# Turning half of the residual by transposing transfers at four stage entries of a fused decoder trunk

## The chip, the core and the metric

The kernel runs on one core of a Trainium2 chip. The core has TensorE (PE in the profile, with its weight loads as PEld), VectorE (DVE), ScalarE (ACT), GpSimd (POOL), and SyncE (SP), which here only issues transfers. All engines run side by side, each through its own list of instructions in order, and wait for one another by semaphores. Transfers that SP issues go through one hardware queue (q1 in the profile), those of POOL through a software queue (q0), and both are served by the same 16 DMA engines. The metric is the device time of one execution in microseconds (us).

## What is computed

A residual stream of 256 tokens and 1024 channels passes two layers; each is a half-step FFN, a mixer, and a half-step FFN, and every one of these six sub-layers reads a normed copy of the stream and adds its normed output to it. The mixer of the first layer is a recurrent block, that of the second is attention whose keys, values and forget gates come from the stream between the layers.

```python
def rms_norm(x, g):
    xf = x.astype(jnp.float32)
    y = xf * lax.rsqrt(jnp.mean(xf * xf, axis=-1, keepdims=True) + EPS)
    return (y * g.astype(jnp.float32)).astype(x.dtype)

def swiglu(x, w_gate, w_up, w_down):
    return (jax.nn.silu(x @ w_gate) * (x @ w_up)) @ w_down

    for layer in range(DEPTH):
        if layer == N_A_LAYERS:
            k, v, c = shared_kv(h, kv_norm_g, w_kv, w_fgate, b_fgate)
        f = swiglu(rms_norm(h, ffn1_pre_g[layer]), ffn1_w_gate[layer], ffn1_w_up[layer], ffn1_w_down[layer])
        h = h + 0.5 * rms_norm(f, ffn1_post_g[layer])
        hn = rms_norm(h, mix_pre_g[layer])
        ...
        h = h + rms_norm(m, mix_post_g[layer])
        f = swiglu(rms_norm(h, ffn2_pre_g[layer]), ffn2_w_gate[layer], ffn2_w_up[layer], ffn2_w_down[layer])
        h = h + 0.5 * rms_norm(f, ffn2_post_g[layer])
    return h
```

All of it is float32. The attention of 16 heads adds to each logit a bias from the running sum of the forget gates, and masks keys later than the query.

## The kernel before

**Tiles.** The 256 tokens are two token tiles, t = 0 and t = 1, of 128. The residual lies in SBUF as `h[0]` and `h[1]`, 128 tokens on the partitions by 1024 channels. A product needs its input the other way round, channels on the partitions: eight k tiles of 128 channels each, numbered 0 to 7. `xhi` and `xlo` hold them, an upper part in a rounded 32-bit format that TensorE takes at full rate and the remainder. Each weight is split in the same way into `whi` (ScalarE, L173) and `wlo` (VectorE, L177), and each product is three matmuls: upper by upper, upper by lower, lower by upper.

**Units.** The weights come in units of 512 KB or so: `load_raw` issues the transfer on SP, `split` makes the two parts. Five raw tiles and nine pairs of parts stand in rotation. The list `items` holds all units in order, and `run` walks it with token tile 0 about seven units ahead of token tile 1. A unit of a projection holds two k tiles and is six matmuls for one token tile. After each unit `tick` is called; `defer(n, f)` has `f` written out n ticks later. TensorE keeps the written order; the other engines' lists are ordered by a scheduler, except where `keep_in_program_order` pins an instruction and `high_priority` pulls a group forward.

**Stage inputs.** When the last product of a sub-layer is done for a token tile, `enter` takes the sum of squares (ScalarE, L205), multiplies by the gain (VectorE, L284), and adds to the residual (L297, one instruction for each half of 512 channels). Three or four ticks later `inputs` turns the new residual: `to_tp` writes four TensorE transposes for each half (L226) into a PSUM bank of the group `gt`; `to_x` then multiplies by the gain of the next norm (VectorE, L234), copies the upper part (ScalarE, L235), and subtracts for the lower part (VectorE, L240). The root of the mean square is left out there and applied to the products' results. There are four such entries:

- entry A: recurrent block to the second FFN of layer 0
- entry B: that FFN to layer 1, where the residual is turned for two inputs, `xhi`/`xlo` and, with another gain, `zhi`/`zlo` for keys, values and gates
- entry C: the first FFN of layer 1 to attention, whose query projection comes first
- entry D: attention to the last FFN

(The entry into the recurrent block goes another way, by `normed_x`.) After entry C the units of the query projection alternate with attention's first steps in an order written by hand (`ATT_ORDER`): logits of token tile 0 (TensorE L1165, then VectorE L1174 with L1178 and L1179 for the row maxima, then ScalarE L1181 for the exponentials, then VectorE L1187 and L1188 for the norm), transposes of the probabilities (L1194), products with the values (L1208). POOL loads 2 MB of bias for token tile 1 at that point (L1009).

**Planes.** The FFN's hidden tiles are already turned by transfer, 48 times: POOL splits the 32-bit words into two planes of 16 bits (L527), SP issues one transposing transfer (`DMA_TRANSPOSE`, L535), and POOL joins the planes again (L540). `planes` (L212), `swap` (L216) and `join` (L220) are the same three steps as functions, used for keys and queries.

Of the kernel before, what the change touches and what calls it, by code (L numbers as in the profile page):

```python
# [17 lines left out]
P = 128  # L18
# [25 lines left out]
def trunk_kernel(ctx: ExitStack, tc: tile.TileContext, A: dict, out: bass.AP):  # L44
# [184 lines left out]
    def x_upper(tp, dest, n):  # L229

        gi, xh, xl = dest
        xg = hpool.tile([P, 4, P], F32, tag="t1", name=nm("xg"), bufs=2)
        g = gT[:, gi + 4 * n:gi + 4 * n + 4].unsqueeze(2).to_broadcast([P, 4, P])
        nc.vector.tensor_tensor(xg, tp.rearrange("p (a b) -> p a b", a=4), g, ALU.mult)  # L234
        nc.scalar.activation(xh[:, 4 * n:4 * n + 4, :], xg, AF.Copy)  # L235
        return xg

    def x_lower(xg, dest, n):
        gi, xh, xl = dest
        nc.vector.tensor_tensor(xl[:, 4 * n:4 * n + 4, :], xg, xh[:, 4 * n:4 * n + 4, :].bitcast(F32), ALU.subtract)  # L240

    def to_x(tps, dest):

        with tc.high_priority():
            xg = [x_upper(tps[n], dest, n) for n in range(2)]
            for n in range(2):
                x_lower(xg[n], dest, n)

    def to_x_tiles(tps, dest):

# [15 lines left out]
    def stat(t):  # L266
        ss = new_ss()
        square_sum(h[t], ss[:, 0:1])
        rs[t] = rstd_of(ss, 1)

    def enter(t, dests, pf, gb, half, last=False, normed=False, wait=3):

        f = 1.0 / 16 if half else 1.0 / 32
        ss = new_ss()
# [27 lines left out]
        if last:  # L302
            return

        def inputs():
            tps = [to_tp(h[t], n) for n in range(2)]
            for dest in dests:
                to_x(tps, dest)
            stat(t)

        def norm():
            with tc.high_priority():
# [179 lines left out]
    def ahead(i, fn):  # L492
# [5 lines left out]
            return prep()  # L498
        items[i] = (both, work)

    def ffn_items(pool_of, wg, wu, wd, post_g, next_dests, last=False, normed=False):
        hid = {}
        sil = {}
# [63 lines left out]
        ahead(i0 + 24, load_gb)  # L567

        def post_down(t, accs):
            enter(t, next_dests(t), accs, box["gb"], True, last, normed)  # L570

        row_items(wd, [P] * 22, lambda t, k: (hid[t][0][:, k, :], hid[t][1][:, k, :]), post_down, 4 if last else 2)
        return i0
# [645 lines left out]
    def post_q(n):  # L1219
        return lambda t, ps: heads_T(ps, t, n, HD ** -0.5, att["q"][t])  # L1220

    for n in range(2):
        proj_items(A["attn_w_q"][0], n * 512, 512, main_x, post_q(n))
    n_q[0] = len(items)
    row_items(A["attn_w_o"][0], [P] * 8, lambda t, k: (att["oh"][t][:, k, :], att["ol"][t][:, k, :]),
              lambda t, accs: enter(t, [main_dest(GI[("ffn2", 1)], t)], accs, gbox["mix1"], False, wait=4),
              rows0=1, late=True)
    ahead(n_q[0] + 2, load_gb("mix1", A["mix_post_g"][1]))
    n_att = len(items)
# [240 lines left out]
```

## Time and profile before

| | us |
|---|---|
| median of 3 runs | 966.03 (965.65 to 968.62) |
| profiled execution, its own time | 965.92 |
| span of that execution in the trace | 964.2 |
| VectorE busy in the span | 640.7 |
| ScalarE busy | 527.6 |
| POOL busy | 218.2 |

The time around the span (1.7 us) is the start and end of the program. Times of day in the rows below are us from the span's start. A row of the timeline gives start, length, engine, line, operation, what is written and read, the shape, how many, and in brackets how long the engine had been idle and what ended the idle time. A matmul's end is modelled: the next one starts before it, so the pace of TensorE is read from start to start.

### The profile page before, as it was taken

How to read it: one execution, taken by the hardware profiler on the slowest of the kernel's cores; microseconds unless marked ns; L12 is line 12 of the kernel's file. 1: busy time of each engine (PE TensorE's matmuls, PEld its weight loads, DVE VectorE, ACT ScalarE, POOL GpSimd, SP SyncE). 2: the span in 40 equal slices, each digit the busy share in tenths (PEclk: the TensorE clock that was granted, in tenths of full speed). 3: DMA queues.
4: the chain of work that ended last, by engine and by line, in shares of the span. 5: the costliest groups of instructions: out<-in, count | busy, mean ns of one | idle time of the engine just before them, and what ended most of it. 6: DMA issues, size and time to landing. Idle time of an engine off the chain costs nothing.

```text
span 964.2 us, 12866 instructions
## 1 busy us (share of the span) xinstructions
PE 955.9 (99%) x4575; PEld 791.3 (82%) x4575; DVE 640.7 (66%) x845; ACT 527.6 (55%) x750; POOL 218.2 (23%) x221
## 2 busy tenths in 40 slices
PE   9999999999999999999999999999999999999997
PEld 6888888898878888888898888888887788888886
DVE  6658674678997666664686566665488876666642
ACT  7546453568886555443565455444366855444431
POOL 2712330130001323230003522234022012232200
PEclk9999999999999999999999999999999999999999
DMA  8787995475346787775558979878773468777731
GB/s 286 226 258 225 256 284 197 142 228 163 119 123 219 209 236 211 205 242 196 135 182 278 253 219 258 230 216 265 226 256 97 133 199 236 207 222 233 223 109 44
DMA packets 148934, 198.79 MB, mean 206 GB/s; under 512 B 67166, under 2 KB 85958, under 8 KB 148742
## 3 DMA queue, kind: packets, MB, share of 16 engines
q1 hardware_dynamic: 146182, 191.06, 65.6%
q0 software_dynamic: 2080, 6.38, 2.1%
q8 instruction: 36, 0.59, 0.2%
q10 hardware_dynamic: 608, 0.53, 0.2%
q14 instruction: 28, 0.23, 0.1%
HBM read 182.19 MB, written 3.16 MB: 192 GB/s over the span
## 4 chain that ended last, share of the span: by engine, by line
PE 95%; DVE 2%; ACT 1%; issue 1%; POOL 0%; DMA 0%; POOLq 0%; DVEq 0%; ACTq 0%
PE mm L428 16%; PE mm L429 16%; PE mm L432 16%; PE mm L183 13%; PE mm L185 13%; PE mm L184 13%; PE gt L795 2%; PE mm L1305 1%; PE mm L190 1%; PE mm L191 1%; PE mm L192 1%; PE gt L226 1%; ACT pe L1181 1%; DVE wlo L177 0%; PE tr L127 0%
## 5 line engine op out<-in xcount | busy, mean ns | idle before, releaser
L177 DVE TENSOR_TENSOR wlo<-raw,whi 128x1024 fp32r<-128x1024 f32 (+5 forms) x329 | 418.0, 1276 | 230.7 <-ACT whi L173 228.3
L173 ACT ACTIVATE whi<-raw 128x1024 fp32r<-128x1024 f32 (+5 forms) x329 | 341.9, 1045 | 308.6 <-PE mm L432 119.2
L428 PE MATMUL mm<-whi,xhi 128*128 128x512 f32 x656 | 256.6, 391 | 0.0
L429 PE MATMUL mm<-wlo,xhi 128*128 128x512 f32 x656 | 255.5, 389 | 0.0
L432 PE MATMUL mm<-whi,xlo 128*128 128x512 f32 x656 | 202.1, 389 | 0.0
L428 PEld LDWEIGHTS mm<-whi,xhi 128*128 128x128 f32 x656 | 123.2, 188 | 25.9 <-issue 0.7
L432 PEld LDWEIGHTS mm<-whi,xlo 128*128 128x128 f32 x656 | 123.1, 188 | 25.8 <-DVE xlo L240 0.2
L429 PEld LDWEIGHTS mm<-wlo,xhi 128*128 128x128 f32 x656 | 123.2, 188 | 25.4 <-DVE wlo L177 0.3
L183 PE MATMUL mm<-whi,hhi 128*128 128x512 f32 x352 | 137.2, 390 | 0.0
L185 PE MATMUL mm<-whi,hlo 128*128 128x512 f32 x352 | 137.0, 389 | 0.0
L184 PE MATMUL mm<-wlo,hhi 128*128 128x512 f32 x352 | 136.9, 389 | 0.0
L540 POOL COPY pl<-prod 128x1024 uint16<-128x1024 uint16 (+1 forms) x48 | 69.9, 1456 | 174.4 <-DMA prod<-pl 174.4
L527 POOL COPY pl<-prod 128x1024 uint16<-128x1024 uint16 (+1 forms) x48 | 66.3, 1382 | 151.9 <-DVE prod L524 86.8
L183 PEld LDWEIGHTS mm<-whi,hhi 128*128 128x128 f32 x352 | 66.1, 188 | 13.7
L185 PEld LDWEIGHTS mm<-whi,hlo 128*128 128x128 f32 x352 | 66.1, 188 | 13.7
L184 PEld LDWEIGHTS mm<-wlo,hhi 128*128 128x128 f32 x352 | 66.1, 188 | 13.6
L198 POOL TENSOR_SCALAR nv<-ss 128x1 f32<-128x1 f32 x22 | 9.6, 437 | 268.7 <-ACT junk L205 268.7
L524 DVE SCALAR_TENSOR_TENSOR prod<-mm,rstd,sil 128x512 f32<-128x512 f32 (+1 forms) x48 | 33.8, 703 | 29.5 <-PE mm L432 25.9
L515 ACT ACTIVATE sil<-mm,rstd 128x512 f32<-128x512 f32 (+1 forms) x48 | 31.0, 649 | 32.9 <-PE mm L432 25.0
L546 DVE TENSOR_TENSOR hlo<-pl,hhi 128x512 fp32r<-128x512 f32 (+1 forms) x48 | 41.2, 858 | 3.7 <-ACT hhi L545 3.7
L183 PE MATMUL mm<-whi,xhi 128*128 128x512 f32 (+1 forms) x112 | 42.8, 382 | 0.0
L185 PE MATMUL mm<-whi,xlo 128*128 128x512 f32 (+1 forms) x112 | 42.5, 379 | 0.0
(223 smaller groups left out, 1054.6 us busy)
## 6 DMA issues: line engine op xcount, KB each, us to landing
raw<-in_ffn_w_down_dram SPq DMA_DIRECT2D x88, 512.0 KB
raw<-in_ffn_w_up_dram SPq DMA_DIRECT2D x80, 512.0 KB
raw<-in_ffn_w_gate_dram SPq DMA_DIRECT2D x78, 512.0 KB
raw<-in_rg_w_in_dram SPq DMA_DIRECT2D x10, 504.0 KB
raw<-in_rg_w_out_dram SPq DMA_DIRECT2D x10, 504.0 KB
raw<-in_ffn_w_gate_dram SPq DMA_DIRECT2D x19, 256.0 KB
raw<-in_ffn_w_up_dram SPq DMA_DIRECT2D x16, 256.0 KB
raw<-in_rg_w_in_dram SPq DMA_DIRECT2D x8, 512.0 KB
```

Source lines behind the costliest of these rows:

```text
L173: up = nc.scalar.activation(hi[:parts, c:c + m], rawv[:, c:c + m], AF.Copy)
L177: nc.vector.tensor_tensor(lo[:parts, c:c + m], rawv[:, c:c + m], hi[:parts, c:c + m].bitcast(F32), ALU.subtract)
L183: nc.tensor.matmul(ps, xh, wh, start=first, stop=False)
L184: nc.tensor.matmul(ps, xh, wl, start=False, stop=False)
L185: nc.tensor.matmul(ps, xl, wh, start=False, stop=last)
L428: nc.tensor.matmul(ps, get_x(t, k)[0], u.hi[:, c], start=k == 0, stop=False)
L429: nc.tensor.matmul(ps, get_x(t, k)[0], u.lo[:, c], start=False, stop=False)
L432: nc.tensor.matmul(ps, get_x(t, k)[1], u.hi[:, c], start=False, stop=k == nk - 1)
L524: nc.vector.scalar_tensor_tensor(pr[:, :nn], ps, rs[t][:, 0:1], s, ALU.mult, ALU.mult)
L527: nc.gpsimd.tensor_copy(halves.rearrange("p (h f) -> p h f", h=2), pr[:, :nn].bitcast(U16).rearrange("p (f h) -> p h f", h=2))
L540: nc.gpsimd.tensor_copy(halves.rearrange("p (f h) -> p h f", h=2), turned.rearrange("p (h a) b -> p h (a b)", h=2))
L546: keep(nc.vector.tensor_tensor(lv, x, hv.bitcast(F32), ALU.subtract))
```

## The change

At entries B, C and D for both token tiles, and at entry A for token tile 1, only the first half (k tiles 0 to 3) is still turned on TensorE. The second half takes the way of the planes. In `enter`, `planes` of `h[t][:, 512:]` on POOL is pulled forward to right behind the residual's update; where `inputs` stands, `swap` issues the transfer on SP; one tick later `join` on POOL; and `turned_to_x`, two ticks behind `inputs` for t = 0 and three for t = 1, multiplies by the gain, copies the upper part and subtracts. Its multiply and copy are pinned in written order. The multiply works in place for the last input, and reads SBUF where L234 reads PSUM. In the changed file these two are lines 258 and 259, and the lines behind are moved by 14 to 29 (L297 is L311 there, L1009 is L1038, L1015 is L1044, L1174 is L1203).

No new memory is taken: the planes and the turned tile lie in tiles that stand empty then, those of the FFN's products (`old_products`, entries B and C), the queries of token tile 0 (`old_q`, entry D), and for t = 1 a tile of the group `t1` and the scratch tile `junk`.

```diff
     def to_x(tps, dest):
 
         with tc.high_priority():
-            xg = [x_upper(tps[n], dest, n) for n in range(2)]
-            for n in range(2):
-                x_lower(xg[n], dest, n)
+            xg = [x_upper(tp, dest, n) for n, tp in enumerate(tps)]
+            for n, v in enumerate(xg):
+                x_lower(v, dest, n)
+
+    def turned_to_x(v, dests, more):
+
+        with tc.high_priority():
+            xs = []
+            for i, (gi, xh, xl) in enumerate(dests):
+                xg = v if i == len(dests) - 1 else more()
+                g = gT[:, gi + 4:gi + 8].unsqueeze(2).to_broadcast([P, 4, P])
+                xs.append(xg.rearrange("p (a b) -> p a b", a=4))
+                tc.keep_in_program_order(
+                    nc.vector.tensor_tensor(xs[i], v.rearrange("p (a b) -> p a b", a=4), g, ALU.mult))
+                tc.keep_in_program_order(nc.scalar.activation(xh[:, 4:, :], xs[i], AF.Copy))
+            for xg, dest in zip(xs, dests):
+                x_lower(xg, dest, 1)
...
-    def enter(t, dests, pf, gb, half, last=False, normed=False, wait=3):
+    def enter(t, dests, pf, gb, half, last=False, normed=False, wait=3, spare=None):
...
+        by_transfer = not normed and (spare or t == 1)
+        if by_transfer:
+            a = spare() if t == 0 else hpool.tile([P, 512], F32, tag="t1", name=nm("hp"), bufs=2)
+            with tc.high_priority():
+                planes(a.bitcast(U16), h[t][:, 512:])
+
         def inputs():
-            tps = [to_tp(h[t], n) for n in range(2)]
+            tps = [to_tp(h[t], n) for n in range(1 if by_transfer else 2)]
             for dest in dests:
                 to_x(tps, dest)
             stat(t)
+            if by_transfer:
+                b = spare() if t == 0 else spool.tile([P, 512], F32, tag="junk", name=nm("ht"), bufs=1)
+                with tc.high_priority():
+                    swap(b.bitcast(U16), a.bitcast(U16))
+                defer(0, lambda: join(a.bitcast(U16).rearrange("p (f h) -> p h f", h=2), b.bitcast(U16)))
+                defer(2 + t, lambda: turned_to_x(a, dests, spare))
...
+    def old_products():
+        return pools["f"].tile([P, 512], F32, tag="prod", name=nm("hp"), bufs=2)
+
...
         def post_down(t, accs):
-            enter(t, next_dests(t), accs, box["gb"], True, last, normed)
+            enter(t, next_dests(t), accs, box["gb"], True, last, normed, spare=old_products)
...
+    q_parts = [1, 0]
+
+    def old_q():
+        return att["q"][0].rearrange("p a b -> p (a b)").rearrange("p (s f) -> p s f", s=2)[:, q_parts.pop(), :]
+
...
-              lambda t, accs: enter(t, [main_dest(GI[("ffn2", 1)], t)], accs, gbox["mix1"], False, wait=4),
+              lambda t, accs: enter(t, [main_dest(GI[("ffn2", 1)], t)], accs, gbox["mix1"], False, wait=4,
+                                    spare=old_q),
```

How instructions stand on three engines, before and now. First POOL at entry C, from the update of token tile 1 on; `nv` and `rstd` are the two steps to a root of a mean square, `bias` is attention's 2 MB, `hp` the planes of the second half and later the joined words, `ht` the turned planes. Before:

```order
L198 TENSOR_SCALAR nv_6331<-ss_6322 128x1
L200 TENSOR_TENSOR rstd_6333<-nv_6331,mhalf 128x1
L1009 DMA bias_6349<-bias1d 128x4096
L198 TENSOR_SCALAR nv_6396<-ss_6393 128x1
L200 TENSOR_TENSOR rstd_6398<-nv_6396,mhalf 128x1
```

Now:

```order
L198 TENSOR_SCALAR nv_6327<-ss_6318 128x1
L200 TENSOR_TENSOR rstd_6329<-nv_6327,mhalf 128x1
L212 COPY hp_6333<-h_75 128x1024
L1038 DMA bias_6347<-bias1d 128x4096
L198 TENSOR_SCALAR nv_6385<-ss_6382 128x1
L220 COPY hp_6333<-ht_6389 128x2x512
L200 TENSOR_TENSOR rstd_6387<-nv_6385,mhalf 128x1
```

The load of the bias is now issued behind the planes of `h[1]` (`h_75`), and the join stands two places behind it.

Second, VectorE in the same place; `htok` is a query block before it is turned, `pe` and `mx` are the logits with their bias and the row maxima. Before:

```order
L1015 TENSOR_SCALAR htok_6406<-mm_6356,rstd_6272 128x512
L240 TENSOR_TENSOR xlo<-xg_6385,xhi 128x4x128
L240 TENSOR_TENSOR xlo<-xg_6388,xhi 128x4x128
L1174 ISA pe_6445,mx_6444<-gt_6433,bias_2950 128x128
L1174 ISA mx_6444 128x1
L1174 ISA pe_6445,mx_6444<-gt_6434,bias_2950 128x128
```

Now:

```order
L1044 TENSOR_SCALAR htok_6397<-mm_6354,rstd_6262 128x512
L240 TENSOR_TENSOR xlo<-xg_6378,xhi 128x4x128
L258 TENSOR_TENSOR hp_6333<-hp_6333,gT 128x512
L1203 ISA pe_6440,mx_6439<-gt_6428,bias_2952 128x128
L1203 ISA mx_6439 128x1
L1203 ISA pe_6440,mx_6439<-gt_6429,bias_2952 128x128
L1203 ISA mx_6439 128x1
L1203 ISA pe_6440,mx_6439<-gt_6428,bias_2952 128x128
L1203 ISA mx_6439 128x1
L240 TENSOR_TENSOR xlo<-hp_6333,xhi 128x4x128
L1044 TENSOR_SCALAR htok_6469<-mm_6400,rstd_6262 128x512
```

The multiply of the transferred half (L258) stands ahead of the first logits, its subtraction and the second query block between the third and the fourth of them.

Third, VectorE at entry B from the inputs of t = 0 to the update of `h[1]`. Before:

```order
L240 TENSOR_TENSOR xlo<-xg_4302,xhi 128x4x128
L240 TENSOR_TENSOR xlo<-xg_4305,xhi 128x4x128
L234 TENSOR_TENSOR xg_4310<-gt_4292,gT 128x512
L234 TENSOR_TENSOR xg_4313<-gt_4297,gT 128x512
L177 TENSOR_TENSOR wlo_4342<-raw_4338,whi_4341 128x720
L240 TENSOR_TENSOR zlo_4246<-xg_4310,zhi_4245 128x4x128
L240 TENSOR_TENSOR zlo_4246<-xg_4313,zhi_4245 128x4x128
L284 TENSOR_TENSOR t_841_4382<-mm_3947,gb_3332 128x512
L284 TENSOR_TENSOR t_842_4384<-mm_3948,gb_3332 128x512
L297 SCALAR_TENSOR_TENSOR h_75<-t_841_4382,rstd_4388,h_75 128x512
L297 SCALAR_TENSOR_TENSOR h_75<-t_842_4384,rstd_4388,h_75 128x512
```

Now:

```order
L177 TENSOR_TENSOR wlo_4333<-raw_4329,whi_4332 128x720
L177 TENSOR_TENSOR wlo_4346<-raw_4342,whi_4345 128x720
L258 TENSOR_TENSOR hp_4349<-hp_4261,gT 128x512
L298 TENSOR_TENSOR t_841_4380<-mm_3946,gb_3331 128x512
L258 TENSOR_TENSOR hp_4261<-hp_4261,gT 128x512
L298 TENSOR_TENSOR t_842_4382<-mm_3947,gb_3331 128x512
L240 TENSOR_TENSOR xlo<-hp_4349,xhi 128x4x128
L240 TENSOR_TENSOR zlo_4245<-hp_4261,zhi_4244 128x4x128
L311 SCALAR_TENSOR_TENSOR h_75<-t_841_4380,rstd_4386,h_75 128x512
L311 SCALAR_TENSOR_TENSOR h_75<-t_842_4382,rstd_4386,h_75 128x512
```

Two multiplies and two subtractions of the transferred half of t = 0, and one more split of a weight, now stand ahead of the update of `h[1]`.

## Prediction

> **What bounds the kernel now.** I read the page's first part and its chain of waits, then the list of all waits, then the timeline around each entry.
>
> ```profile
> PE 955.9 (99%) x4575; PEld 791.3 (82%) x4575; DVE 640.7 (66%) x845; ACT 527.6 (55%) x750; POOL 218.2 (23%) x221
> PEclk9999999999999999999999999999999999999999
> PE 95%; DVE 2%; ACT 1%; issue 1%; POOL 0%; DMA 0%; POOLq 0%; DVEq 0%; ACTq 0%
> PE tr L127 <- PEq L1455: 0.8, 1, 0.8
> ```
>
> TensorE is busy 99% of the span and 95% of the chain that ended last; its longest single wait is 0.8 us. So the time moves in two ways only: by what TensorE no longer executes, and by each place where it now has to wait.
>
> **What is removed.** Seven entries of a token tile (A once, B, C and D twice) lose four transposes each.
>
> ```profile
> 713.56 1.04 PE L226 MATMUL gt<-ident,h 128*128 128x128 f32 x8
> 714.35 0.47 PE L428 MATMUL mm<-whi,xhi 128*128 128x512 f32 x1
> 714.66 0.39 PE L429 MATMUL mm<-wlo,xhi 128*128 128x512 f32 x1
> 714.89 0.39 PE L428 MATMUL mm<-whi,xhi 128*128 128x512 f32 x1
> ```
>
> Two matmuls start 0.23 apart (714.66 to 714.89). From the first transpose to the second matmul behind the eight it is 714.66 - 713.56 = 1.10; less 0.23 for the matmul between, 0.87 for eight, 0.109 each. 28 x 0.109 = **-3.05 us**. This is all that the change can gain: an execution without a new wait would be 0.32% shorter, and about 0.3% is what a measurement can tell from no change. [...]
>
> **What the new way costs.** The nearest rows are of attention's queries and of the hidden tiles, which go through the same three steps.
>
> ```profile
> 730.78 1.90 POOL L212 COPY pl<-htok 128x1024 uint16<-128x1024 uint16 x1 [14.64 <-DVE htok L1015]
> 732.70 1.24 SPq L216 DMA_TRANSPOSE htok<-pl  x1
> 735.82 1.69 POOL L220 COPY qT<-htok 128x1024 uint16<-128x1024 uint16 x1 [3.14 <-DMA htok<-pl]
> L540 POOL COPY pl<-prod 128x1024 uint16<-128x1024 uint16 (+1 forms) x48 | 69.9, 1456 | 174.4 <-DMA prod<-pl 174.4
> L234 DVE TENSOR_TENSOR xg<-gt,gT 128x512 f32<-128x512 f32 x4 | 2.6, 683 | 0.0
> L235 ACT ACTIVATE xhi<-xg 128x512 fp32r<-128x512 f32 x4 | 2.5, 634 | 2.1 <-DVE xg L234 2.1
> L240 DVE TENSOR_TENSOR xlo<-xg,xhi 128x512 fp32r<-128x512 f32 x4 | 2.6, 684 | 0.0
> ```
>
> Planes 1.4 to 1.9; from the issue to the start of the join 735.82 - 732.70 = 3.1 on a quiet queue; join 1.46; multiply, copy, subtraction about 0.65 each (VectorE's last 0.04 overlap). Some 8 us from the residual to k tiles 4 to 7, against 0.5 us of transposes. I went through the seven entries by what is due when.
>
> At A, at B for t = 1, at C for t = 0 and at D the half is wanted later than that. The tightest is C, t = 0:
>
> ```profile
> 701.11 1.41 DVE L297 SCALAR_TENSOR_TENSOR h<-t,rstd,h 128x512 f32<-128x512 f32 x2 [0.38 <-POOL rstd L200]
> 712.19 0.39 PE L428 MATMUL mm<-whi,xhi 128*128 128x512 f32 x1
> ```
>
> The update ends at 702.5, the first matmul on k tile 4 stands at 712.2: 9.7 us for some 8, and a little queueing on VectorE still fits. I cost these at nothing, covered by units on k tiles 0 to 3; a transfer late by more than 1 us would show as a wait of L428.
>
> **Entry B, t = 0.** Here the transfer lands early enough (the update ends at 474.6), but the work behind it is late.
>
> ```profile
> 473.20 1.41 DVE L297 SCALAR_TENSOR_TENSOR h<-t,rstd,h 128x512 f32<-128x512 f32 x2 [0.36 <-POOL rstd L200]
> 481.22 0.90 DVE L177 TENSOR_TENSOR wlo<-raw,whi 128x720 fp32r<-128x720 f32 x1
> 482.94 1.46 ACT L173 ACTIVATE whi<-raw 128x720 fp32r<-128x720 f32 x2
> 484.31 0.39 PE L428 MATMUL mm<-whi,xhi 128*128 128x512 f32 x1
> 485.68 1.03 PE L226 MATMUL gt<-ident,h 128*128 128x128 f32 x8
> ```
>
> VectorE's split of 481.22 ends at 482.1; two multiplies of the second half (1.3) are gone ahead of it, and one more split of 0.9 follows: VectorE reaches the first L258 around 481.7, and ScalarE's copy for it then falls behind the splits that run from 482.94 to 484.4, or ahead of the second of them. Its end is about 484.5; TensorE, 0.44 early by four transposes, wants k tile 4 at 483.87. I take a wait of 0.65. On VectorE, L258 twice and L240 twice now stand ahead of the two updates of `h[1]`: from 481.7, L258, product, L258, product, two L240 and the first update are seven instructions of 0.65, so the first half of `h[1]` is ready near 486.4, where TensorE would turn it at 485.9: another 0.6. **+1.25 us**; bounds 0 (the scheduler's list runs dry earlier) and 2.5 (the copy waits behind both splits and the second update is waited for too).
>
> **Entry C, t = 1.** This decides.
>
> ```profile
> 711.73 1.42 DVE L297 SCALAR_TENSOR_TENSOR h<-t,rstd,h 128x512 f32<-128x512 f32 x2
> 711.71 0.63 POOL L1009 DMA_DIRECT2D bias<-bias1d  x1
> 714.34 1.43 SPq L164 DMA_DIRECT2D raw<-in_attn_w_o_dram  x2
> bias<-bias1d POOLq DMA_DIRECT2D x1, 2048.0 KB, 11.7
> 714.00:722.00 8.00, 8.00 (x52) 6.51 (x51) 4.81 (x10) 2.21 (x5) 1.57 (x2) 1.00 0.98 374
> 722.00:725.00 3.00, 3.00 (x15) 2.47 (x14) 2.66 (x19) 0.89 (x5) 0.00 (x0) 1.00 0.57 234
> ```
>
> The update ends at 713.15, planes by 714.65. In POOL's list the 2 MB load of the bias stands right behind the planes, so it moves from 711.71 to about 714.65, and SP issues `swap` at about 714.8, behind a 512 KB weight load of 714.34. In the last two rows (DMA share and GB/s are the last columns) the 16 DMA engines are filled at 0.98 and 374 GB/s up to 722, and at 0.57 behind it: the load, issued at 711.71, holds them for 722 - 711.7 = 10.3 us. The trace holds the same collision once:
>
> ```profile
> 577.74 1.04 POOL L527 COPY pl<-prod 128x1024 uint16<-128x1024 uint16 x1 [2.74 <-DVE prod L524]
> 578.73 1.14 POOL L988 DMA_DIRECT2D bias1d<-crows  x1
> 578.81 1.24 SPq L535 DMA_TRANSPOSE prod<-pl  x1
> 589.99 2.20 POOL L540 COPY pl<-prod 128x1024 uint16<-128x1024 uint16 x1 [10.13 <-DMA prod<-pl]
> ```
>
> POOL's load of 1 MB was issued 0.08 us ahead of a transposing transfer, and the join followed 589.99 - 578.81 = 11.2 us behind the issue, where the quiet one took 3.1. I take the join's start J as the end of the load, 714.65 + 10.3 = 725.0. Bounds: 719.2, quiet with the weight load ahead (512 KB at 374 GB/s, 1.4 us, then 3.1), and 725.9 by the 11.2 of the row. I choose near the upper one, as the collision is the nearest row by far. [...]
>
> On VectorE L258 waits for the join, and all logits (L1174) of token tile 0 stand behind it, with a query block (`htok`, L1015) and the exponentials of ScalarE in turn.
>
> ```profile
> 721.66 0.29 DVE L1174 CUSTOM_DVE_ANT_0 pe<-gt,bias 128x128 f32<-128x128 f32 x1 [3.19 <-PE gt L1165]
> 721.88 0.29 DVE L1174 CUSTOM_DVE_ANT_0 pe<-gt,bias 128x128 f32<-128x128 f32 x1
> L1015 DVE TENSOR_SCALAR htok<-mm,rstd 128x512 f32<-128x512 f32 x3 | 2.2, 746 | 0.2 <-PE mm L432 0.2
> L1181 ACT ACTIVATE pe<-pe,mx 128x128 f32<-128x128 f32 x16 | 6.2, 391 | 6.4 <-DVE mx L1179 6.4
> L1188 DVE TENSOR_TENSOR pe<-pe,sm 128x512 f32<-128x512 f32 x4 | 2.8, 692 | 0.1
> 725.78 0.60 PE L1028 MATMUL tr<-ident,htok 128*128 128x128 f32 x4
> 727.60 0.60 PE L1194 MATMUL tr<-ident,pe 128*128 128x128 f32 x4
> ```
>
> From J on: join 1.46, L258 0.64, three logits at 0.21, subtraction 0.65, `htok` 0.67, the remaining logits and maxima about 0.9, three exponentials at 0.39, the copy of the turned query block, which is next on ScalarE, 0.58, the fourth exponential 0.5 with its sum, reciprocal 0.2, norm 0.69; with some 0.1 of handing over, J + 8.2. TensorE wants that norm at L1194, 727.60 less 0.87 for the eight transposes that both tiles saved at this entry, 726.7. The loss is J + 8.2 - 726.7 = J - 718.5 = **+6.5 us**, in two waits: `htok` is ready at J + 4.1 = 729.1 where L1028 stands at 724.9, about 4.2, and the rest, 2.3, at L1194. Bounds: 1.1 (J = 719.2 gives 0.7, and one split that now stands ahead of the exponentials on ScalarE some 0.4 more) and 7.4.
>
> **Sum.** 964.2 - 3.05 + 1.25 + 6.5 = 968.9 of span; 965.92 - 964.2 = 1.7 lie around it, and the median is 0.1 above the profiled execution: **970.7 us**, 0.5% slower.
>
> **The rivals.**
>
> *The transfer passes the load* (not slower). If the 16 engines serve SP's queue as if POOL's load were not there, J is 719.2 and the loss at C 1.1: 964.2 - 3.05 + 1.25 + 1.1 + 1.8 = 965.3. It decides at J = 720.3, where the loss equals the 1.8 us that are left of the gain; up to J = 723.2 the result still lies within 0.3%. For it speaks that 2 MB in 10.3 us are 204 GB/s of the 374, so that the weight loads of SP's queue went on beside POOL's load; against it the row of 589.99. If moreover B hides, the time is 963.0, the floor.
>
> [...]
>
> *The clock falls in the new stalls.* Two waits of 4.2 and 2.3 us lie close together. No wait of TensorE in this trace is over 0.8 us and the granted clock (PEclk) stands at 9 tenths or more in every slice, so nothing here shows what follows a longer one. [...]
>
> *The half is hidden everywhere.* Then 963.0; it asks both B and C to be wrong.
>
> **How the numbers follow.** The forecast, a transfer held behind the load, has 0.55 with 968.9 to 973 of its own; the clock beside it 0.06; in turn 0.15; passing the load 0.17; hidden everywhere 0.07. The first two are slower by over 0.3% (above 968.9): 0.61. The next two, 967.0 and 965.3, lie within it: 0.32. The last is about at 0.3% faster (963.1): 0.07. The range leaves out the hidden case and the uppermost end: 965.0 to 973.2, the latter being 970.7 with the upper bounds of B and C added (1.25 and 0.9) and 0.35 for the spread.
>
> **What would show it.** In the changed kernel's profile: at C, t = 1, POOL's join (L220) idle for about 10 us on the transfer; TensorE waiting about 4 us for `htok` at the query block's transposes and about 2 for `pe` at those of the probabilities, where before it waited for nothing; at B, t = 0, waits of half a microsecond for ScalarE's copy (L259) and for `h`; none at A, D and C, t = 0; 28 fewer matmuls on L226. I am wrong if that join starts 3 to 6 us behind its issue, if TensorE's waits stay under 3 us in all, or if L428 waits at an entry that I cost at nothing.

## The result, and the profile after

| | before | changed |
|---|---|---|
| median, us | 966.03 | 977.73 |
| range of 5 runs, us | 965.56 to 968.62 | 976.81 to 979.68 |
| profiled execution, its own time | 965.92 | 977.03 |
| its span | 964.2 | 975.3 |

The ratio is 1.0123, with a 95% interval of 1.0111 to 1.0135: slower by 11.7 us where 4.7 were forecast, and outside the range. First the page of the changed kernel (busy time; granted clock in 40 slices; the chain that ended last), then its list of TensorE's waits (us in total, times, longest).

```profile
PE 956.1 (98%) x4547; PEld 788.2 (81%) x4547; DVE 652.4 (67%) x845; ACT 527.8 (54%) x750; POOL 244.9 (25%) x235
PEclk9999999999999999999999999999998999999999
PE 89%; DVE 3%; issue 2%; DMA 2%; ACT 2%; POOL 1%; POOLq 0%; DVEq 0%; ACTq 0%
```

```profile
PE tr L1057 <- DVE htok L1044: 7.1, 1, 7.1
PE mm L454 <- ACT xhi L259: 1.7, 2, 1.0
...
PE gt L226 <- DVE h L311: 0.5, 1, 0.5
PE mm L458 <- DVE xlo L240: 0.5, 1, 0.5
PE tr L1223 <- DVE pe L1217: 0.4, 1, 0.4
```

TensorE makes 28 matmuls fewer, as it should, and its share of the chain falls from 95% to 89%. The waits in these five rows are new and come to 10.2 us. One more number stands out: VectorE has the same 845 instructions and is busy 652.4 us instead of 640.7. The chain of the transfer itself was priced; this was not.

**Where the time went.** Each matmul of the changed kernel can be paired with the same matmul of the kernel before. The difference of their start times, read between the entries, is TensorE's delay; a step in it is a gain or a loss of that place. "Four transposes fewer" is the gain of each token tile there, a negative number. (The time before the first product scatters by some 0.3 us from execution to execution, the -0.2 here.)

| place | delay ahead of it | behind it | four transposes fewer, per tile | loss there | forecast |
|---|---|---|---|---|---|
| A, t = 1 | -0.20 | -0.60 | -0.40 | 0 | 0 |
| B, both tiles | -0.60 | 1.56 | -0.45, -0.43 | 3.0 | 1.25 |
| C, t = 0 | 1.56 | 2.37 | -0.44 | 1.25 | 0 |
| C, t = 1 | 2.37 | 11.55 | -0.34 | 9.5 | 6.5 |
| D, both tiles | 11.6 | 10.99 | -0.41, -0.43 | 0.2 | 0 |

The gain is 2.9 us (forecast 3.05), the losses are 14.0 (forecast 7.75).

**Entry C, t = 1.** POOL's, SP's, VectorE's and TensorE's timelines there (start, length, then what ran, and in brackets the idle time ahead and what ended it):

```profile
715.23 1.41 DVE L311 SCALAR_TENSOR_TENSOR h<-t,rstd,h 128x512 f32<-128x512 f32 x2
716.70 1.97 POOL L212 COPY hp<-h 128x1024 uint16<-128x1024 uint16 x1 [2.18 <-DVE h L311]
718.61 0.63 POOL L1038 DMA_DIRECT2D bias<-bias1d  x1
718.69 1.24 SPq L216 DMA_TRANSPOSE ht<-hp  x1
731.00 1.31 POOL L220 COPY hp<-ht 128x1024 uint16<-128x1024 uint16 x1 [11.18 <-DMA ht<-hp]
732.35 0.69 DVE L258 TENSOR_TENSOR hp<-hp,gT 128x512 f32<-128x512 f32 x1 [11.35 <-POOL hp L220]
732.96 0.28 DVE L1203 CUSTOM_DVE_ANT_0 pe<-gt,bias 128x128 f32<-128x128 f32 x1
734.35 0.75 DVE L1044 TENSOR_SCALAR htok<-mm,rstd 128x512 f32<-128x512 f32 x1
735.15 1.11 PE L1057 MATMUL tr<-ident,htok 128*128 128x128 f32 x4 [7.13 <-DVE htok L1044]
739.12 0.63 PE L1223 MATMUL tr<-ident,pe 128*128 128x128 f32 x4 [0.43 <-DVE pe L1217]
```

The predicted chain is there link by link: the load and the transfer 0.08 us apart, a join that waits, L258 behind it, the logits and `htok` behind L258, TensorE behind `htok`. From the join's start to L1223 it is 739.12 - 731.00 = 8.1 us (8.2 were forecast). But the join starts at 731.0 and not at 725.0.

**VectorE in two stretches.** Each row has the stretch, its length, then the busy time and the number of instructions of PE, PEld, DVE, ACT and POOL, then granted clock, DMA share and GB/s. The same windows around entry B and entry C, before and then changed:

```profile
472.50:490.00 17.50, 17.50 (x90) 14.99 (x89) 17.14 (x26) 13.10 (x22) 3.53 (x8) 1.00 0.43 132
703.00:721.00 18.00, 18.00 (x96) 14.89 (x96) 15.47 (x20) 12.67 (x21) 4.34 (x7) 1.00 0.82 295
```

```profile
472.50:490.00 17.50, 15.47 (x72) 12.04 (x71) 17.41 (x22) 11.57 (x20) 9.09 (x9) 1.00 0.51 146
703.00:721.00 18.00, 17.27 (x82) 13.51 (x80) 18.00 (x20) 12.88 (x20) 9.14 (x9) 1.00 0.69 222
```

Busy two thirds of the whole span, VectorE was busy 17.14 of 17.5 us at entry B before the change: it had no time to lose exactly there. Now it is fuller, and in the same 17.5 us it gets through 22 instructions instead of 26. Why each takes longer is seen beside POOL's copies, at entry B of the changed kernel, with two undisturbed splits of the kernel before in a fence of their own:

```profile
474.07 1.97 POOL L212 COPY hp<-h 128x1024 uint16<-128x1024 uint16 x1 [1.51 <-DVE h L311]
473.93 3.19 DVE L177 TENSOR_TENSOR wlo<-raw,whi 128x1024 fp32r<-128x1024 f32 x2
479.17 1.78 POOL L220 COPY hp<-hp 128x1024 uint16<-128x1024 uint16 x1 [1.32 <-DMA hp<-hp]
479.66 1.78 DVE L240 TENSOR_TENSOR zlo<-xg,zhi 128x512 fp32r<-128x512 f32 x1
483.00 0.68 DVE L258 TENSOR_TENSOR hp<-hp,gT 128x512 f32<-128x512 f32 x1
483.71 0.63 ACT L259 ACTIVATE xhi<-hp 128x512 fp32r<-128x512 f32 x1 [0.45 <-DVE hp L258]
484.39 0.50 PE L454 MATMUL mm<-whi,xhi 128*128 128x512 f32 x1 [0.96 <-ACT xhi L259]
```

```profile
713.06 2.35 DVE L177 TENSOR_TENSOR wlo<-raw,whi 128x1024 fp32r<-128x1024 f32 x2
```

Two splits take 3.19 us where two alone take 2.35, and a subtraction of 0.68 takes 1.78: it begins while POOL's join runs and ends 0.5 us behind the join's end. The transferred half had been joined at 480.95; VectorE, without a gap since 472.6, comes to it at 483.0.

### The profile page after: what moved, and what is told of

It reads as the page before. It is cut to its first block, busy times and chain, and to the rows that moved or that the text cites. A ratio compares the mean times of both kernels' runs of the same rounds, so it can differ in the third digit from the quotient of the medians.

```text
span 975.3 us, 12833 instructions
## 1 busy us (share of the span) xinstructions
PE 956.1 (98%) x4547; PEld 788.2 (81%) x4547; DVE 652.4 (67%) x845; ACT 527.8 (54%) x750; POOL 244.9 (25%) x235
## 4 chain that ended last, share of the span: by engine, by line
PE 89%; DVE 3%; issue 2%; DMA 2%; ACT 2%; POOL 1%; POOLq 0%; DVEq 0%; ACTq 0%
PE mm L454 15%; PE mm L458 15%; PE mm L455 15%; PE mm L183 12%; PE mm L185 12%; PE mm L184 12%; PE gt L824 2%; DMA ht<-hp 1%; PE mm L1340 1%; PE mm L190 1%; PE mm L191 1%; PE mm L192 1%; DVE wlo L177 1%; ACT pe L1210 1%; DVE pe L1203 0%
## 5 line engine op out<-in xcount | busy, mean ns | idle before, releaser
L177 DVE TENSOR_TENSOR wlo<-raw,whi 128x1024 fp32r<-128x1024 f32 (+5 forms) x329 | 429.2, 1310 | 212.0 <-ACT whi L173 209.9
L198 POOL TENSOR_SCALAR nv<-ss 128x1 f32<-128x1 f32 x22 | 11.5, 525 | 234.1 <-ACT junk L205 234.1
```

What stands on the lines that cost most here:

```text
L177: nc.vector.tensor_tensor(lo[:parts, c:c + m], rawv[:, c:c + m], hi[:parts, c:c + m].bitcast(F32), ALU.subtract)
```

## Experiments

Each experiment is a change to the changed kernel. "Delay" is TensorE's, as in the table above; "load" is the 2 MB load of attention's bias.

**1. The load behind the join.**

```diff
     def att_rows():
...
-        tc.keep_in_program_order(nc.gpsimd.dma_start(att["bias1"], kv["bias1"]))
+    def att_bias():
+        tc.keep_in_program_order(nc.gpsimd.dma_start(att["bias1"], kv["bias1"]))
...
-    for c in ATT_ORDER.split():
+    for j, c in enumerate(ATT_ORDER.split()):
+        if j == 5:
+            att_bias()
```

> The changed kernel, but POOL issues the 2 MB load of the bias behind the join at entry C, t = 1, instead of ahead of the transposing transfer. Theory (the load holds the transfer): the join starts 3 to 5 us behind the issue instead of 12.3, the wait of 7.1 us for htok and the slow matmuls behind it are gone, a rest of 0 to 1.5 us is left at the transposes of the probabilities: 968 to 970.5 us. Rival (the place of the multiply and of the logits on VectorE costs this, whatever the load does): 975 us or more.

970.91 us (ratio 1.0056, 1.0041 to 1.0071). POOL's and SP's timeline, then the load's row in the list of DMA issues (KB, us to landing):

```profile
718.64 1.24 SPq L216 DMA_TRANSPOSE ht<-hp  x1
723.66 1.34 POOL L220 COPY hp<-ht 128x1024 uint16<-128x1024 uint16 x1 [3.24 <-DMA ht<-hp]
724.91 0.63 POOL L1041 DMA_DIRECT2D bias<-bias1d  x1
```

```profile
bias<-bias1d POOLq DMA_DIRECT2D x1, 2048.0 KB, 8.4
```

The join starts 5.0 us behind the issue, the load itself lands after 8.4 us instead of 11.5, and the wait for `htok` falls from 7.1 to 1.2 us. 977.73 - 970.91 makes the collision worth 6.8 us. The rest, 970.9 - 966.0 = 4.9, is left without it. The time is 0.4 us above the expected range, and a wait for `htok` of 1.2 us is left where none was expected.

**2. The load in smaller pieces.**

```diff
-        tc.keep_in_program_order(nc.gpsimd.dma_start(att["bias1"], kv["bias1"]))
+        to, fr = (v.rearrange("p (a b) s -> p b a s", b=2) for v in (att["bias1"], kv["bias1"]))
+        for b in range(2):
+            tc.keep_in_program_order(nc.gpsimd.dma_start(to[:, b], fr[:, b]))
```

> The changed kernel, but the load of the bias, at its place ahead of the transfer, consists of 2048 pieces of 1 KB instead of 128 of 16 KB (two DMAs of 1 MB), all bytes the same. Theory (each DMA engine serves the two queues one piece in turn, so that a 256-byte piece of the transfer waits for a 16 KB piece of the load): the join starts 4 to 7 us behind the issue; 968.5 to 972. Rival (the transfer counts as done only when the load has ended, or the bytes share the bandwidth equally whatever the pieces are): the join stays 10 us or more behind; 975 or more.

981.53 us (1.0155, 1.0138 to 1.0172). Against both numbers of the theory, and within those of the rival:

```profile
719.33 1.24 SPq L216 DMA_TRANSPOSE ht<-hp  x1
734.13 1.32 POOL L220 COPY hp<-ht 128x1024 uint16<-128x1024 uint16 x1 [12.41 <-DMA ht<-hp]
```

```profile
bias<-bias1d POOLq DMA_DIRECT2D x2, 1024.0 KB, 18.5
```

The join comes 14.8 us behind the issue, later than before, and each half of the load takes 18.5 us in the mean until it has landed. The trace has 512 records of 4 KB for the load and not 2048 of 1 KB; so the pieces were smaller by 4, not 16. A plain alternation, one piece of each queue in turn, should still have freed the transfer earlier. Most of its pieces did move earlier. Here are the DMA records between 720 and 726 us, in this kernel and then in the changed one; most of those under 512 bytes are the transfer's 1024 pieces:

```profile
DMA packets 1010, 0.93 MB, mean 156 GB/s; under 512 B 833, under 2 KB 833, under 8 KB 1010
```

```profile
DMA packets 250, 1.83 MB, mean 306 GB/s; under 512 B 73, under 2 KB 73, under 8 KB 161
```

But the last piece of the transfer ended 11.7 us behind the issue in both kernels (at 731.06 and 730.34), and the join started 3.1 us behind that piece instead of 0.7. So the forecast of the theory falls, though the first pieces went as it says; what holds up the last pieces and the end is open. The rival's first half falls too, and with it the prediction's reading that the join waits for the whole load: the join starts at 734.13, the halves of the load landed at 736.4 and 740.1.

**3. Half of the load ahead, half behind the join.**

```diff
-        tc.keep_in_program_order(nc.gpsimd.dma_start(att["bias1"], kv["bias1"]))
+        att_bias(0)
+    def att_bias(n):
+        tc.keep_in_program_order(nc.gpsimd.dma_start(att["bias1"][:, 8 * n:8 * n + 8], kv["bias1"][:, 8 * n:8 * n + 8]))
...
+        if j == 5:
+            att_bias(1)
```

> The changed kernel, but the load of the bias is cut in two: heads 0 to 7 (1 MB, 128 pieces of 8 KB) at its place ahead of the transfer, heads 8 to 15 behind the join. Theory (the two transfers hold each other up for as long as both have pieces left): the join starts 6.5 to 9 us behind the issue, half of the excess; 971.5 to 975 us. Rival (a load in POOL's queue beside a transposing transfer costs about the same whatever its size): 11 us or more behind; 976 or more.

975.74 us (1.0099, 1.0085 to 1.0114).

```profile
718.71 1.24 SPq L216 DMA_TRANSPOSE ht<-hp  x1
727.78 1.32 POOL L220 COPY hp<-ht 128x1024 uint16<-128x1024 uint16 x1 [7.29 <-DMA ht<-hp]
```

9.1 us behind the issue, with 5.0 for no load and 12.3 for all of it: half the bytes cost 56% of the excess, 0.1 us above the expected range, so the cost grows with the bytes and is not fixed. The time is above the range for another reason, the clock (below).

**4. The load in the transfer's own queue, directly behind it.**

```diff
-        tc.keep_in_program_order(nc.gpsimd.dma_start(att["bias1"], kv["bias1"]))
+    def att_bias():
+        tc.keep_in_program_order(nc.sync.dma_start(att["bias1"], kv["bias1"]))
...
+        if j == 5:
+            att_bias()
```

> The changed kernel, but SP issues the load of the bias, into the same queue as the transposing transfer and directly behind it. Theory (what holds the transfer up is that pieces of two queues alternate; in one queue the load waits its turn): the join starts 4.5 to 5.5 us behind the issue though 2 MB follow it at once, 969 to 971.5 us as with the load behind the join. Rival (2 MB in flight beside it cost the same in any queue): the join starts 9 us or more behind, 974 or more.

971.18 us (1.0057, 1.0041 to 1.0074).

```profile
718.66 1.24 SPq L216 DMA_TRANSPOSE ht<-hp  x1
720.07 0.45 SPq L1041 DMA_DIRECT2D bias<-bias1d  x1
723.63 1.34 POOL L220 COPY hp<-ht 128x1024 uint16<-128x1024 uint16 x1 [3.19 <-DMA ht<-hp]
```

The same 2 MB, issued 1.4 us behind the transfer, cost it nothing: 5.0 us, as without them. In the one queue the load's first piece began at 722.85, as the transfer's last was about to end (723.12), so the load waited its turn. But two things differ from the changed kernel, the queue and the order: there the load was issued 0.08 us ahead of the transfer. No run has POOL's load issued behind the transfer, so which of the two decides is not shown.

**5. The load from ScalarE's queue.**

```diff
-        tc.keep_in_program_order(nc.gpsimd.dma_start(att["bias1"], kv["bias1"]))
+        tc.keep_in_program_order(nc.scalar.dma_start(att["bias1"], kv["bias1"]))
```

> The changed kernel, but ScalarE issues the load of the bias, into its own hardware queue, ahead of the transfer; with this the scheduler puts VectorE's multiply of the half behind the logits of token tile 0 and not ahead of them. Theory (a load from any other queue holds the transfer up): the join starts 9 us or more behind its issue, the wait for htok is gone, and TensorE waits 4 to 6 us for the half itself: 973 to 976 us. Rival (only POOL's queue does this): the join starts 4 to 6 us behind, 967 to 970 us.

973.68 us (1.0075, 1.006 to 1.0091). On the queue it says nothing: ScalarE issued the load at 714.3, and the swap, which waits for the scratch tile, came only at 724.1, 9.8 us behind it (in experiment 1 the load landed after 8.4). Its join followed 6.4 us behind, between the ranges of theory and rival. But the join, at 730.6, was as late as in the changed kernel, and VectorE had the multiply behind the logits this time. TensorE did not wait for `htok`; it waited 4.2 us for the half itself. The time is 4 us less than in the changed kernel for the same lateness of the join. The logits, which no longer queue behind L258, are the likely reason; the place of the load differs too.

**6. C, t = 1, on TensorE.**

```diff
+    entries = [["A", "B", "C", "D"] for _ in range(2)]
+    on_pe = ('C1',)
...
         by_transfer = not normed and (spare or t == 1)
+        if not normed and f"{entries[t].pop(0)}{t}" in on_pe:
+            by_transfer = False
```

> The changed kernel with token tile 1 of entry C turned whole on TensorE, as before the change. Theory: all of the loss at that place goes, 9.5 us of delay between 714 and 728 less the 0.43 of its four transposes; what is left is entry B (2.6) and token tile 0 of C (1.1) less the transposes saved: 967 to 968. Rival (what is late there is late anyway and shows up at the next wait): over 970.

969.85 us (1.0038, 1.0023 to 1.0053). The stall is gone, the delay goes from 3.7 to 4.1 over the whole place. The time is 1.9 us above the expected range. Part of it is the clock, which in this execution fell at entry B. Windows there (busy times as above, then granted clock, DMA share, GB/s):

```profile
484.00:486.00 2.00, 1.19 (x4) 0.67 (x4) 2.00 (x4) 1.25 (x2) 0.60 (x2) 1.00 0.90 290
486.00:488.00 2.00, 1.26 (x4) 0.63 (x5) 2.00 (x4) 0.00 (x0) 0.00 (x0) 0.69 0.64 207
488.00:490.00 2.00, 2.00 (x8) 1.71 (x7) 2.00 (x4) 1.15 (x2) 1.66 (x2) 0.50 0.26 76
490.00:492.00 2.00, 2.00 (x12) 1.85 (x11) 0.71 (x1) 1.08 (x2) 1.36 (x2) 0.96 0.45 147
```

TensorE, busy 2.45 of 4 us with three short waits, is then granted half its clock for some 3.4 us. Its delay grows by 3.2 us over entry B, 1.0 more than in the changed kernel, in whose profiled execution much the same waits left the clock at 1.00. Such waits therefore have a cost of their own in some executions and none in others.

**7. POOL's copies alone.** All transposes on TensorE, no transfer, but planes and a second copy into a tile that nothing reads.

```diff
-            tps = [to_tp(h[t], n) for n in range(1 if by_transfer else 2)]
+            if by_transfer:
+                b = spare() if t == 0 else spool.tile([P, 512], F32, tag="junk", name=nm("ht"), bufs=1)
+                join(b.bitcast(U16).rearrange("p (f h) -> p h f", h=2), a.bitcast(U16))
+            tps = [to_tp(h[t], n) for n in range(2)]
...
-                    swap(b.bitcast(U16), a.bitcast(U16))
-                defer(0, lambda: join(a.bitcast(U16).rearrange("p (f h) -> p h f", h=2), b.bitcast(U16)))
-                defer(2 + t, lambda: turned_to_x(a, dests, spare))
```

> All eight transposes on TensorE as before the change, but POOL still makes the two copies of the planes' way at the seven entries (planes, and a second copy with the join's pattern into an empty tile that nothing reads); no transposing transfer, no L258 and L259. Theory (a POOL copy stretches the VectorE instruction beside it by about 0.85 us): VectorE's busy time goes from 641 to 650 to 653 us with the same number of instructions, nearly all of it in the splits of L177, and the time rises to 967 to 970. Rival (VectorE is slower in the changed kernel because the multiply reads SBUF, or by its place): busy time stays at 641 to 643 and the time at 966.

968.53 us (1.0029, 1.0018 to 1.004). Its page: busy times, and the group of the splits (busy and mean ns), whose row before the change follows.

```profile
PE 956.6 (99%) x4575; PEld 791.2 (82%) x4575; DVE 648.9 (67%) x845; ACT 527.0 (55%) x750; POOL 249.2 (26%) x235
L177 DVE TENSOR_TENSOR wlo<-raw,whi 128x1024 fp32r<-128x1024 f32 (+5 forms) x329 | 425.9, 1301 | 218.7 <-ACT whi L173 217.6
```

```profile
L177 DVE TENSOR_TENSOR wlo<-raw,whi 128x1024 fp32r<-128x1024 f32 (+5 forms) x329 | 418.0, 1276 | 230.7 <-ACT whi L173 228.3
```

VectorE is busy 8.2 us longer with the same instructions, 7.9 of it in the splits: 0.6 us for each of 14 copies (0.85 were expected, and a busy time of 650 or more). The kernel takes 2.5 us more, but not all of that is VectorE's. TensorE's delay grows by 0.8 us at entry B, by nothing at C for t = 0, by 0.6 at C for t = 1, and by 1.55 at D for t = 1, where this row stands:

```profile
786.73 1.06 ACT L205 ACTIVATE junk<-h 128x1024 bf16<-128x1024 f32 x1 [6.03 <-POOL ht L220]
```

ScalarE's sum of squares writes the scratch tile into which POOL makes its unused second copy, and had to wait for that copy; the copy of the input behind it was then late. That is the tile's doing and not the stretching's.

**8. The copies on ScalarE.** Base: experiment 1; a copy of one column by POOL, which waits for the join, keeps the load behind it.

```diff
-                planes(a.bitcast(U16), h[t][:, 512:])
+                nc.scalar.activation(a.bitcast(U16).rearrange("p (h f) -> p h f", h=2),
+                                     h[t][:, 512:].bitcast(U16).rearrange("p (f h) -> p h f", h=2), AF.Copy)
...
-                defer(0, lambda: join(a.bitcast(U16).rearrange("p (f h) -> p h f", h=2), b.bitcast(U16)))
+                defer(0, lambda: tc.keep_in_program_order(nc.scalar.activation(
+                    a.bitcast(U16).rearrange("p (f h) -> p h f", h=2), b.bitcast(U16).rearrange("p (h f) -> p h f", h=2), AF.Copy)))
```

> The kernel with the load behind the join (970.9 us), but ScalarE makes the two copies (planes, join) of the seven entries instead of POOL; the load of the bias still follows the join of entry C, t = 1. Theory (a POOL copy holds up the VectorE instruction beside it, a ScalarE copy does not): VectorE's busy time falls from 649 to 641 to 644 us and entries B and C lose about 2 us less: 967.5 to 969.5. Rival (the order on the lists is what makes B and C late, and ScalarE's list gets 14 copies of 1 us more): 970.5 or more.

969.58 us (1.004, 1.0024 to 1.0056), between the two.

```profile
PE 954.4 (99%) x4547; PEld 787.6 (81%) x4547; DVE 642.8 (66%) x845; ACT 541.5 (56%) x764; POOL 221.0 (23%) x222
```

VectorE's time falls from the 649.3 of experiment 1 to 642.8 as the theory has it, so it is POOL that stretches it. But entry B loses 3.1 us as before: now ScalarE is late with the copy (TensorE's waits for it come to 2.6 us), and VectorE waits for ScalarE. Both are needed at once there. C, t = 0, loses 0.9 instead of 1.25. So this run shows whose copies stretch VectorE, and not what the stretching costs at entry B.

**9. B, t = 0, on TensorE.** Base: experiment 1, with the edit of experiment 6 and another name.

```diff
+    on_pe = ('B0',)
```

> The kernel with the load behind the join (970.9 us), but token tile 0 of entry B is turned whole on TensorE. Theory (two multiplies, two subtractions and two stretched instructions on VectorE make the upper half of t = 0 and then h[1] late): of the 3.5 us lost at entry B 2.5 to 3.5 go, 0.43 for the four transposes comes back: 967.7 to 969. Rival (t = 1 of entry B costs most of it): 970 or more.

968.5 us (1.0027, 1.0018 to 1.0036): 2.4 us less. Entry B then changes the delay from -0.51 to -0.86, which is the gain of t = 1 with 0.1 lost. Nearly all that entry B loses is lost by t = 0.

**10. The multiply one tick earlier for t = 0.** Base: experiment 1.

```diff
-                defer(2 + t, lambda: turned_to_x(a, dests, spare))
+                defer(1 + 2 * t, lambda: turned_to_x(a, dests, spare))
```

> The kernel with the load behind the join (970.9 us), but for t = 0 the multiply of the transferred half is written one tick earlier, so that on VectorE one split fewer stands ahead of it at entries B and C. Theory (the half has been joined for 2 us when VectorE comes to it, so its place on the list is part of the delay): the waits of TensorE for ScalarE's copy at B and C (0.7 and 1.0 us) go, that for h[1] at B stays: 968.5 to 970. Rival (VectorE has too much to do there in any order, by the stretched instructions and the added ones): the waits only change their place, 970.5 or more.

970.6 us (1.0045, 1.0032 to 1.0059), no change. The waits for ScalarE's copy fall from 1.7 to 0.5 us, and those of L226 for `h` rise from 0.5 to 2.0. At C both splits still stand ahead of the update of `h[1]`, which is no earlier for it. At B the update is 0.8 us earlier, reckoned from that of `h[0]` (13.2 us behind it instead of 14.0), but TensorE, which the half no longer holds up, waits 1.1 us for it. The rival holds: the place on VectorE's list mainly decides who waits for it.

**11. Only the four places that nobody waits for:** A and B for t = 1, D for both tiles; the rest on TensorE, by the edit of experiment 6.

```diff
+    on_pe = ('B0', 'C0', 'C1')
```

> Only the four places whose half was not waited for go by transfer: A and B for t = 1, D for both tiles. Theory: four times four transposes are saved, 1.74 us, and POOL's copies beside VectorE give back 0 to 1: 964.3 to 965.5 us, faster than before. Rival (a half that is not waited for still costs as much as it saves, by what POOL's copies do to VectorE): 966 or more.

964.82 us, ratio 0.9988 (0.9979 to 0.9997): faster than before by 1.1 us, within the expected range. VectorE is busy 641.3 us, hardly more than before, and no wait of TensorE is left that the change made. This beats both kernels, by little.

**12. The same, and C, t = 0, with the earlier multiply of experiment 10.**

```diff
+    on_pe = ('B0', 'C1')
```

> By transfer: A and B for t = 1, D for both tiles (964.8 us with these four), and now C for t = 0, with the multiply one tick earlier. Theory (its half is late only by the place of the multiply): 0.43 us of transposes more are saved, less 0 to 0.4 at h[1] of entry C: 964.3 to 965. Rival (POOL's two copies there hold VectorE up by 2 us and the update of h[1] with it): 965.5 to 966.5.

966.5 us (1.0002, 0.9993 to 1.0011). Turning this one half by transfer saves 0.44 us and costs 2.1 (the delay goes from -0.89 behind its transposes to 1.16 behind those of t = 1): TensorE waits 0.9 for `h[1]`, whose update VectorE reaches late, and 0.2 for the half. Beside POOL's two copies there VectorE's splits take 3.19 us for two and 2.31 for one, instead of 2.35 and 1.22: 1.9 us, the 2 us of the rival. The rival holds, and this is the run that shows most directly what the stretching costs.

## Why the prediction was wrong, step by step

- **What bounds the kernel, and the gain.** Right. TensorE's transposes are worth 0.10 to 0.11 us each, 2.9 us in all. (The record of one of them on L226 is 0.27 us long; the next starts before it ends, so the starts and not the lengths give the price.)
- **A and D, hidden.** Right: A shows no loss, D 0.2 us.
- **The price of the new way.** This is the step that failed. "Planes 1.4 to 1.9 ... join 1.46" was taken as time of POOL alone, on a chain that VectorE meets only at L258. In fact the splits and subtractions on VectorE, which have two inputs in SBUF, are held up when they start beside such a copy (two splits took 3.19 us instead of 2.35, a subtraction 1.78 instead of 0.68). With that, L258 of entry B stands at 483.0 and not at 481.7, although the update of `h[0]` was 0.6 us earlier: 1.9 late, and the two long rows there are 0.84 and 1.1 us too long. VectorE has no gap there before or after the change, so the times add up: the update of `h[1]` is 2.2 us later than before (486.60 and 484.44), by 1.9 of stretching and 0.8 of the split that was priced, less the 0.6. That POOL's copies stretch VectorE is shown by experiments 7 and 8, from both sides, and that this costs TensorE time by experiment 12. How much of the 3.0 us at B is the stretching's is read from these rows and not shown by a run: experiment 7, in which the copies stand alone, lost 0.8 there, and experiment 8 moved the wait to ScalarE.
- **C, t = 0, "9.7 us for some 8, ... still fits".** Wrong by the same step. The transfer was in time (joined at 710.75); VectorE, with two stretched rows of splits ahead (again 0.84 and 1.1 us), came to L258 at 712.83, and TensorE waited. Cover was counted in the time of the transfer, not in the time that VectorE had to spare. Entries B and C lost 3.0 and 1.25 us where 1.25 and 0 were forecast.
- **C, t = 1.** The mechanism was right and was shown by experiments 1, 3 and 4; the size, J = 725.0, was 6 us too early. The update of `h[1]` ended at 716.6 instead of 713.15 (3.5: the 1.56 of delay ahead of entry C and the 1.9 by which VectorE's rows are stretched there), planes took 1.97 instead of 1.5 (0.5), and the join followed the load's issue by 12.4 instead of 10.3 (2.1): the load's 10.3 us were read from a stretch in which no transposing transfer ran beside it; beside one it landed after 11.5, and the join came 0.9 behind that. TensorE would have reached L1194 some 2.0 us behind the kernel before, where 0.87 ahead was reckoned, so 6.0 - 2.9 = 3.1 of it are loss.
- **The split between the two waits.** 4.2 and 2.3 us were forecast, 7.1 and 0.4 came. The clock is the reason that the second is so short:

```profile
733.00:735.00 2.00, 0.00 (x0) 0.00 (x0) 1.94 (x9) 1.58 (x2) 0.00 (x0) 0.50 0.00 0
735.00:737.00 2.00, 1.85 (x7) 1.66 (x8) 2.00 (x14) 1.09 (x6) 0.00 (x0) 0.50 0.02 4
737.00:739.00 2.00, 1.69 (x5) 0.91 (x3) 1.53 (x5) 2.00 (x10) 0.00 (x0) 0.65 0.38 45
739.00:741.00 2.00, 1.88 (x10) 1.44 (x10) 1.31 (x3) 2.00 (x7) 0.00 (x0) 1.00 0.56 217
```

- **The rival of the clock** was right as a mechanism: granted 0.50 from 731.6, during the stall, to 738.4. It cost nothing here, because TensorE would have waited for `pe` until 739.1 at any clock; the six slow matmuls only filled that wait. In experiment 3, where no wait followed, the same fall took the delay from 7.5 to 9.9 us.
- **The rivals of the transfer.** "Passes the load" and "served in turn" (965.3 and 967.0) are refuted by 12.3 us between issue and join. No run shows the term behind the 967.0; the join came 9.1 us behind the issue with half of the load beside the transfer (experiment 3) and 12.3 with all of it.
- **The range.** The side was right, slower. The range added the upper bounds of B and of C, t = 1, but both bounds were too low (B lost 3.0 where 2.5 was the bound, and J came at 731.0 where 725.9 was), and C, t = 0, had no term at all. One cause, VectorE's stretched list, has a part in all three. Of the 7.0 us between the forecast and the median, 6.25 are these losses and D's, 0.15 the smaller gain, and 0.6 the median's distance from the profiled execution, 0.7 here where 0.1 was taken.

## What to carry to other kernels

Before work is moved off the bounding engine, look at the busy time of the engines that take it over in the very stretch where they take it over, not over the span: VectorE was free a third of the span and 0.4 us of 17.5 at entry B. A copy on POOL was not free for VectorE here: splits, which have two inputs in SBUF, took 1.65 us beside one instead of 1.22. And the chain through POOL, VectorE and ScalarE was as late as the fullest of their lists: at entry B the half was joined at 480.95, and VectorE came to it at 483.0. Issue a transposing transfer ahead of a bulk load in one queue, as in experiment 4, or keep the two apart in time, as in experiment 1: in both the join came 5.0 us behind the issue instead of 12.3. Where the gain per place is 0.4 us, move only the places that nobody waits for.

## What the runs showed of the hardware

**POOL beside VectorE.** Splits and subtractions, VectorE instructions with two inputs in SBUF, ended late when they started while POOL copied in SBUF. The trace of before already held it, in rows that the prediction did not use:

```profile
335.94 1.36 POOL L540 COPY pl<-prod 128x1024 uint16<-128x1024 uint16 x1 [2.13 <-DMA prod<-pl]
336.46 1.86 DVE L177 TENSOR_TENSOR wlo<-raw,whi 128x1024 fp32r<-128x1024 f32 x1 [1.44 <-ACT whi L173]
```

The split starts 0.52 us into the copy and ends 1.02 behind its end, at 338.32. Of the full-size splits of that trace, 53 began during such a copy and took 1.65 us in the mean; the other 239 took 1.22. Wherever in the copy they began, all 53 ended 1.01 to 1.22 us behind its end, nearly the 1.22 us that a split takes alone; why, no run here shows. Multiplies that read PSUM and one input in SBUF were not held up: five of L234 began during a copy in the changed kernel and took 0.68 to 0.69 us, as without one. Experiment 8 agrees on whose copies do it: VectorE was busy 642.8 us with ScalarE's copies and 649.3 with POOL's.

**A transposing transfer beside a load of another queue.** Alone they took 5.0 (with a weight load ahead in its queue) and 8.4 us, together 12.3 and 11.5. With four times as many pieces of the load it was 14.8, and 18.5 for each half. Most of the transfer's pieces moved earlier then (833 records under 512 bytes between 720 and 726 us instead of 73), and the join still came later. Why is open.

**The clock.** With single waits of 5.2, 7.1 and 9.6 us (experiment 3, the changed kernel, experiment 2) TensorE was granted 0.50 for 6.8, 6.8 and 10.2 us around the wait's end; with one of 1.2 us (experiment 1) it kept 1.00. The execution with one of 4.2 us (experiment 5) had a mean granted clock of 0.997, those of the kernel before beside it 0.998 to 1.000. Three waits of together 1.8 us within 4 us lowered it to 0.50 for some 3.4 us in one execution (experiment 6), and three of 2.0 us left it at 1.00 in another (the changed kernel). What decides there, the runs do not show.

**The rounded parts.** The pace that the text on the tiles calls full rate was 0.227 us from start to start for 512 columns in the kernel before (L428, L429 and L432), at a granted clock of 1.00. A transpose of 128 columns of unrounded float32 (L226) took 0.109.
